# Two units of a query weight moved off POOL's scaling, and one weight split set ahead of a normed row

## The chip, the cores and the metric

The kernel runs on one core of a Trainium2 chip. The core has five engines that each take their own instructions in order: PE multiplies matrices, DVE and ACT work element by element and read the PSUM banks that PE writes, POOL works element by element in SBUF, and SP issues the transfers. The metric is the device time of one execution in microseconds (us), a median over runs.

## The reference

Two layers of an encoder on x of 512 rows and 1024 columns, in float32. Layer 0 mixes tokens with a banded attention (12 heads, each query sees 128 rows to either side) and a memory attention (4 heads over 256 memory rows); layer 1 has a global attention in place of the banded one. Each layer does this:

```
h    = rms_norm(x, g_mix_pre[i]);  proj = h @ w_in[i]      # q, k, v, q of the memory heads
o    = concat(token mixer, memory attention) @ w_o[i];     x = x + rms_norm(o, g_mix_post[i])
h    = rms_norm(x, g_ffn_pre[i]);  gu = h @ w_gate_up[i]
f    = (silu(gu[:, :2816]) * gu[:, 2816:]) @ w_down[i];    x = x + rms_norm(f, g_ffn_post[i])
```

## The kernel before

**Products of split operands.** Every float32 operand of a large product is split into a rounded part `hi` and a rest `lo = x - hi`, and `mm3` (L268) makes three matmuls from them (L270 to L272). A weight comes as a *unit* of 128x1024 elements: a transfer into `raw` (L224, three buffers), then `hi` (`whi`) and `lo` (`wlo`, four buffers each). The next transfer into a `raw` buffer can start once the unit in it has been split.

**Who splits.** `unit` has an argument `side`, a number of two bits that comes from the table `PACE`. In layer 0 the units of `w_in` and of the memory weights are scaled by the gain of the norm on the way (`g`). With the low bit set, POOL scales `raw` in place, 256 columns at a time (L236), and POOL also makes `lo` (L282); with the low bit clear, the scaling lies in the split itself (`split_scaled`, L286): `hi` by ACT (L292) or, with the high bit set, by POOL (L290), and `lo` by DVE (L293). With the low bit set, `hi` comes from ACT (L280) or, with the high bit, from POOL (L278).

**The first mixer.** `mixer` lays out pieces of work by due times from `PACE`. The query weights are eight units, `qw[2c + z]` for four blocks c of 256 columns and two halves z. While PE still projects queries and memory keys, it begins the scores (L548, L549) of the first heads. For a head, DVE adds the mask (L554), ACT takes the exponential (L560), POOL divides by the sums (`p`, L599) and PE transposes the result (L609). A tile of queries is scaled by ACT (L512), turned by four DVE operations (the rotary, L422 to L425), split by ACT (L280) and DVE (L284), and transposed (L524). The memory keys go through `keys` (L404): two batches of transposes (L409, L414), copied out by ACT (L411) and DVE (L415); the second batch has a single PSUM bank (`pv`).

**The start of the gate/up product.** In `ffn` the first two blocks f of 128 hidden columns are computed plainly, with four units (f, b), b for gate and up. They are laid between the last rows of the output projection. `plain` multiplies a unit; between the units stand `late.pop(2)` and `late.pop(3)`, which turn the third and fourth 128 rows of the normed h (`Forms.turn`: L149 transposes, L280 and L284 split, L159 copies, L162 subtracts). Row 3 of h is made by `post_norm`: DVE adds the residual (L742), ACT takes squares (L303), POOL makes the factor r with three operations on one column (L308, L313, L314), DVE multiplies (L756).

**The order.** PE's instructions stand as written. On the other engines a scheduler orders them by a priority that follows the order of the code; `high_priority(n)` moves what is recorded under it n places forward.

Of the kernel before, what the change touches and what calls it, by code (L numbers as in the profile page):

```python
# [31 lines left out]
WPART = 2  # L32
BIG = 1e37
NFILL = 3
LOTS = ((0, 8), (8, 14), (14, 22))

PACE = [{'lag': 1.692, 'vlag': 0.479, 'jstep': 0.213, 'kstep': 0.375, 'klag': 0.742, 'qoff': [0.212, 0.126, 0.099], 'qlag': 1.02, 'late': 0.6, 'moff': -0.235, 'mdur': 0.562, 'mlag': 0.697, 'kw': [0, 0, 2, 0], 'mw': [2, 1, 1, 0], 'qw': [1, 0, 0, 1, 3, 3, 3, 3], 'hoff': 0, 'ow': [10.3, 10.8, 12.2, 13.2], 'ox': 11.4, 'od': 0.3, 'hstep': 0.872, 'hlag': 1.742, 'hjstep': 0.135, 'hvlag': 0.751, 'owm': [0, 0, 0, 0, 0, 0, 0, 0], 'q0step': 0.27, 'q0off': -0.032, 'q0lag': 0.919, 'm0off': -0.078, 'm0dur': 0.002, 'm0lead': 1.887, 'mlead': 1.201, 'qlead': 0.921, 'q0lead': 1.555, 'qstep': 1.002, 'tw': [0, 0, 0, 0, 0, 0, 0, 0], 'h2off': 0}, {'lag': 1.824, 'vlag': 0.535, 'jstep': 0.218, 'kstep': 0.777, 'klag': 1.715, 'qoff': [-0.027, -0.162, -0.027], 'qlag': 1.189, 'late': 2.15, 'moff': -0.088, 'mdur': 0.384, 'mlag': 1.205, 'kw': [0, 0, 0, 0], 'mw': [0, 0, 0, 0], 'qw': [0, 0, 0, 0, 0, 3, 1, 1], 'hoff': 0, 'ow': [10.2, 10.7, 12.2, 13.2], 'ox': 11.3, 'od': 0.3, 'hstep': 0.946, 'hlag': 1.847, 'hjstep': 0.295, 'hvlag': 0.568, 'owm': [0, 0, 0, 0, 0, 0, 0, 0], 'q0step': 0.718, 'q0off': -0.018, 'q0lag': 1.136, 'm0off': -1.059, 'm0dur': 0.171, 'm0lead': 2.465, 'mlead': 3.162, 'qlead': 1.895, 'q0lead': 1.42, 'qstep': 0.998, 'tw': [0, 0, 0, 0, 0, 0, 0, 0], 'h2off': 0.016}]

# [139 lines left out]
class Trunk:  # L180
# [84 lines left out]
    def side(self, l, key, u):  # L265
        return PACE[l][key][u]

# [381 lines left out]
    def mixer(self, l, mkp, late, tokp):  # L649
        nc = self.nc  # L650
        pc = PACE[l]
        if l == 0:
# [112 lines left out]
    def heads_out(self, l, put, xw, xs, x0, dx):  # L765
# [7 lines left out]
        def part(k):  # L773
            if k % 4 == 0:
                self.th[k // 4] = [self.hp.tile([P, 4, S], F32R, tag=f"h{k // 4}{z}", name="th", bufs=1)
                                   for z in range(2)]
            self.split(self.th[k // 4][0][:, k % 4], self.th[k // 4][1][:, k % 4], self.tok[:, k],
                       self.side(l, "tw", k))

        def prod(k, t):  # L780
            if t == len(self.po):
                self.po.append(self.bank())
                if t == 2:
                    self.held = self.turns.pop()
            self.prod(self.po[t], self.heads, KD, k, t, self.wo[k // 2])

        for k in range(KD):
            put(max(xs[k], x0 + (NFILL * k - 1.5) * dx) if k < NH // 2 else xs[k], lambda k=k: part(k))
        for k in range(NH // 2):
            for t in range(NFILL):  # L790
                put(max(x0 + (NFILL * k + t) * dx, xs[k] + 0.001 * (t + 1)), lambda k=k, t=t: prod(k, t))

# [3 lines left out]
    def mix_out(self, l, forms, resid, dst):  # L796
# [3 lines left out]
        g, gn = self.gain(a["g_mix_post"][l], "gpost"), self.gain(a["g_ffn_pre"][l], "gpre")  # L800
        po = self.po + [self.bank() for _ in range(NT - NFILL)]
        self.turns.insert(1, self.held)
        w1 = []
        for u in range(4):
            for k in (2 * u, 2 * u + 1):
                for t in range(0 if k >= NH // 2 else NFILL, NT):
                    self.prod(po[t], self.heads, KD, k, t, self.wo[u])
# [97 lines left out]
    def ffn(self, l, pools, forms, late, done):  # L905
# [6 lines left out]
        w, raw, st = {}, {}, {}  # L912

        def units(f):
            w[f] = [self.unit(self.a["wgu"][l, f, b]) for b in range(2)]

        def plain(f, b, q, pg):
            c = slice(256 * q, 256 * q + 256)
            for k in range(KD):
                s = slice(k * P, (k + 1) * P)  # L920
                self.mm3(pg[b][:, c], w[f][b][0][:, s], w[f][b][1][:, s], forms.plain(0, k, q), forms.plain(1, k, q),
                         k == 0, k == KD - 1)
# [75 lines left out]
        def body(f, pos, nxt, nxt2, fill):  # L998
            d = st[f]
            x = d["x"]  # L1000
            seven(f, x, "c", 1, "S2", False)
            copy(f, "u2", x)
            y = self.tagged("t")[:, :256]
            seven(f, y, "c", 0, "nS1", True)
            copy(f, "p5", y)
            if nxt is not None:
                load_b(nxt)
                prep_c(nxt)
                p1(nxt)
            else:  # L1010
                fill[0]()
            seven(f, x, "b", 1 - 1, "S3", False)
            c = d["cc"] = temp("c")
            nc.vector.tensor_add(c[:, 256:], x, d["p5"])
            if nxt is not None:
                p2(nxt)
            else:
                fill[1]()
            if nxt2 is not None:
                prep_a(nxt2)  # L1020
            seven(f, y, "b", 1, "S4", False)
            nc.vector.tensor_add(c[:, :256], y, d["u2"])
            if nxt is not None:
                prep_b(nxt)
            seven(f, x, "d", 0, "A22", False)
            s = d["s"]
            nc.scalar.activation(s[:, 256:], x, AF.Silu)
            nc.vector.tensor_mul(s, s, c)
            F[f] = hidden(pos)
            nc.scalar.activation(F[f][0], s, AF.Copy, scale=-1.0)  # L1030
            nc.vector.scalar_tensor_tensor(F[f][1], s, -1.0, F[f][0].bitcast(F32), op0=OP.mult, op1=OP.subtract)
            if nxt is not None:
                prep_d(nxt)
            st.pop(f)

        pgs = []
        for f in range(2):
            units(f)
            pgs.append([self.bank() for _ in range(2)])
            for b in range(2):  # L1040
                plain(f, b, 0, pgs[f])
                if f == 0 and b == 1:
                    late.pop(2)()
                if f == 1 and b == 0:
                    late.pop(3)()
# [13 lines left out]

        for c, (f0, f1) in enumerate(LOTS):  # L1060
            fs = list(range(f0, f1))
# [21 lines left out]
            for i, f in enumerate(gs):  # L1083
                more = gs[i + 1:] + [None, None]
                body(f, f - f0, more[0], more[1], [first, second])
            if c < len(LOTS) - 1:
                self.down(get, self.a["wd"][l], fs, c, o, head)
# [158 lines left out]
```

## Time and profile before

| | us |
|---|---|
| median of 3 runs | 1124.72 |
| lowest, highest | 1124.1, 1125.98 |
| the profiled execution | 1125.38 |
| its span, first to last instruction | 1123.6 |
| PE busy | 1096.6 (98%) |
| DVE, ACT, POOL busy | 844.3 (75%), 660.8 (59%), 203.8 (18%) |

In 40 slices of the span the granted clock of PE is at its top (9 of 9 tenths) in every one. PE's digits are 9 in all slices but the first (8) and the last (7). POOL's digits are high only in the first seven slices, that is in the first 200 us, where it splits weights and scales probabilities.

### The profile page before, as it was taken

The numbers are of one execution on the slowest core, as the hardware profiler recorded it, in microseconds if no ns is written. First come the engines' busy times: TensorE is split into PE (matmuls) and PEld (weight loads), VectorE is DVE, ScalarE is ACT, GpSimd is POOL, SyncE is SP. The second block draws the span as 40 slices with busy tenths as digits, with TensorE's granted clock in tenths as the row PEclk, the third lists the DMA queues.
The fourth block names the chain that finished last, engine by engine and source line by source line (L and its number), as shares of the span: only waits on it lengthen the run. The fifth ranks groups of instructions, "written<-read, shape, count | busy, mean of one in ns | idle before, by whom it ended". The sixth has DMA issues, their size and how long they took to land.

```text
span 1123.6 us, 19533 instructions
## 1 busy us (share of the span) xinstructions
PE 1096.6 (98%) x7463; PEld 1003.6 (89%) x7463; DVE 844.3 (75%) x1431; ACT 660.8 (59%) x1343; POOL 203.8 (18%) x348
## 2 busy tenths in 40 slices
PE   8999999999999999999999999999999999999997
PEld 7889988899889989998898888878999899899985
DVE  5688885899557867885788998758996478669854
ACT  6678984666445634663467878756665255345631
POOL 5693331102000000000343543312000000000001
PEclk9999999999999999999999999999999999999999
DMA  6521015443753382325543221145136223423243
GB/s 237 194 81 47 20 57 206 169 132 114 243 180 112 112 283 76 112 79 195 179 150 113 76 76 39 38 150 188 39 113 217 65 76 114 149 62 103 85 166 112
DMA packets 38685, 139.29 MB, mean 124 GB/s; under 512 B 4416, under 2 KB 4800, under 8 KB 38464
## 3 DMA queue, kind: packets, MB, share of 16 engines
q1 hardware_dynamic: 38448, 137.91, 36.4%
q8 instruction: 58, 0.95, 0.3%
q14 instruction: 35, 0.29, 0.1%
q10 hardware_dynamic: 144, 0.14, 0.0%
HBM read 119.16 MB, written 18.87 MB: 123 GB/s over the span
## 4 chain that ended last, share of the span: by engine, by line
PE 68%; DVE 6%; ACT 3%; POOL 2%; issue 2%; DVEq 0%; POOLq 0%; ACTq 0%
PE ps L978 12%; PE ps L979 12%; PE ps L980 12%; PE ps L271 9%; PE ps L270 9%; PE ps L272 9%; PE tp L609 1%; PE o L624 1%; PE o L623 1%; PE s L548 1%; DVE nm L559 1%; PE s L549 1%; DVE wlo L284 1%; POOL r L299 1%; ACT whi L280 1%
## 5 line engine op out<-in xcount | busy, mean ns | idle before, releaser
L280 ACT ACTIVATE whi<-raw 128x1024 fp32r<-128x1024 f32 (+2 forms) x186 | 157.9, 863 | 185.2 <-PE ps L980 81.8
L284 DVE TENSOR_TENSOR wlo<-raw,whi 128x1024 fp32r<-128x1024 f32 (+2 forms) x178 | 175.9, 998 | 74.8 <-ACT whi L280 71.7
L978 PE MATMUL ps<-sf,whi 128*128 128x256 f32 x640 | 179.9, 281 | 0.2
L979 PE MATMUL ps<-sf,wlo 128*128 128x256 f32 x640 | 179.7, 281 | 0.0
L980 PE MATMUL ps<-sf,whi 128*128 128x256 f32 x640 | 179.7, 281 | 0.0
L270 PE MATMUL ps<-whi,f 128*128 128x512 f32 x352 | 137.2, 390 | 0.0
L271 PE MATMUL ps<-wlo,f 128*128 128x512 f32 x352 | 137.1, 390 | 0.0
L272 PE MATMUL ps<-whi,f 128*128 128x512 f32 x352 | 137.0, 389 | 0.0
L980 PE MATMUL ps<-a,whi 128*128 128x256 f32 x480 | 134.4, 280 | 0.0
L978 PE MATMUL ps<-a,whi 128*128 128x256 f32 x480 | 134.3, 280 | 0.0
L979 PE MATMUL ps<-a,wlo 128*128 128x256 f32 x480 | 133.8, 279 | 0.0
L978 PEld LDWEIGHTS ps<-sf,whi 128*128 128x128 f32 x640 | 121.1, 189 | 1.1 <-ACT p L984 0.6
L979 PEld LDWEIGHTS ps<-sf,wlo 128*128 128x128 f32 x640 | 121.4, 190 | 0.5
L980 PEld LDWEIGHTS ps<-sf,whi 128*128 128x128 f32 x640 | 121.4, 190 | 0.0
L308 POOL TENSOR_SCALAR e<-sso 128x1 f32<-128x1 f32 x8 | 3.4, 424 | 566.1 <-ACT junk L303 565.9
L270 PE MATMUL ps<-whi,hT 128*128 128x256 f32 (+1 forms) x320 | 98.8, 309 | 0.9 <-ACT whi L292 0.9
L271 PE MATMUL ps<-wlo,hT 128*128 128x256 f32 (+1 forms) x320 | 93.9, 294 | 2.6 <-DVE wlo L284 1.9
L599 POOL TENSOR_SCALAR p<-p,rd 128x256 f32<-128x256 f32 (+2 forms) x128 | 78.2, 630 | 99.8 <-DVE rd L596 50.3
L272 PE MATMUL ps<-whi,hT 128*128 128x256 f32 (+1 forms) x320 | 93.7, 293 | 0.0
L979 PEld LDWEIGHTS ps<-a,wlo 128*128 128x128 f32 x480 | 90.5, 188 | 0.2
L978 PEld LDWEIGHTS ps<-a,whi 128*128 128x128 f32 x480 | 90.4, 188 | 0.2
L980 PEld LDWEIGHTS ps<-a,whi 128*128 128x128 f32 x480 | 90.1, 188 | 0.0
(201 smaller groups left out, 2735.0 us busy)
## 6 DMA issues: line engine op xcount, KB each, us to landing
raw<-in_wgu_dram SPq DMA_DIRECT2D x48, 512.0 KB, 4.4
raw<-in_wd_dram SPq DMA_DIRECT2D x44, 512.0 KB, 4.4
rb<-in_wgu_dram SPq DMA_DIRECT2D x40, 512.0 KB, 3.6
raw<-in_wo_dram SPq DMA_DIRECT2D x17, 512.0 KB, 3.6
raw<-in_wq_dram SPq DMA_DIRECT2D x16, 512.0 KB, 5.0
xt<-x SPq DMA_DIRECT2D x12, 512.0 KB, 4.5
raw<-in_wm_dram SPq DMA_DIRECT2D x8, 512.0 KB, 4.3
x<-y SPq DMA_DIRECT2D x8, 512.0 KB, 3.0
```

What stands on the lines that cost most here:

```text
L270: mm(out, lh, rh, start=first, stop=False)
L271: mm(out, lh, rl, start=False, stop=False)
L272: mm(out, ll, rh, start=False, stop=last)
L280: nc.scalar.activation(hi, src, AF.Copy)
L284: nc.vector.tensor_sub(lo, src, hi.bitcast(F32))
L299: g.tensor_tensor(r, r, self.mhalf[:, :r.shape[1]], op=OP.pow)
L548: nc.tensor.matmul(s[:, :n], qi, hd["ka"]()[:, k0 * P:k1 * P], start=True, stop=False)
L549: nc.tensor.matmul(s[:, :n], qi, hd["kb"]()[:, k0 * P:k1 * P], start=False, stop=True)
L599: self.pooled = nc.gpsimd.tensor_scalar(hd["p"][z][:, :n], hd["p"][z][:, :n], rd[:, z:z + 1], 1.0, op0=OP.mult, op1=OP.mult)
L978: mm(out, wh[:, s], rh, start=start and k == 0, stop=False, skip_group_check=True)
L979: mm(out, wl[:, s], rh, start=False, stop=False, skip_group_check=True)
L980: mm(out, wh[:, s], rl, start=False, stop=k == 3, skip_group_check=True)
```

## The change

In layer 0's `qw`, unit 3 (c = 1, z = 1) goes from side 1 to side 0, and unit 4 (c = 2, z = 0) from side 3 to side 2. In `ffn`, in both layers, the unit (f, b) = (1, 1) is no longer recorded by `units(1)` but right behind it, with a priority moved forward by 150 places. The two `PACE` lines below are cut to the field that differs.

```diff
+EARLY = 150
...
-'qw': [1, 0, 0, 1, 3, 3, 3, 3]
+'qw': [1, 0, 0, 0, 2, 3, 3, 3]
...
         def units(f):
-            w[f] = [self.unit(self.a["wgu"][l, f, b]) for b in range(2)]
+            w[f] = [self.unit(self.a["wgu"][l, f, b]) for b in range(2 - f)]
...
         for f in range(2):
             units(f)
+            if f:
+                with self.tc.high_priority(EARLY):
+                    w[f].append(self.unit(self.a["wgu"][l, f, 1]))
             pgs.append([self.bank() for _ in range(2)])
```

PE's and SP's instructions stand as before. On POOL, in the first mixer, this is the stretch before. `raw_711` is unit 3, `raw_1087` unit 4, `raw_1139`, `raw_1597` and `raw_1630` are units 5 to 7; `k2_816` and `k2_841` are the memory keys, `p_888` the first head's probabilities.

```order
L236 TENSOR_SCALAR raw_711<-raw_711,cst_87 128x256 x4
L236 TENSOR_SCALAR raw_1087<-raw_1087,cst_87 128x256 x4
L282 TENSOR_TENSOR wlo_713<-raw_711,whi_712 128x512 x2
L278 TENSOR_SCALAR whi_1088<-raw_1087 128x512 x2
L282 TENSOR_TENSOR wlo_1089<-raw_1087,whi_1088 128x512 x2
L236 TENSOR_SCALAR raw_1139<-raw_1139,cst_87 128x256 x3
L402 TENSOR_SCALAR k2_816<-k2_816 128x4x64
L236 TENSOR_SCALAR raw_1139<-raw_1139,cst_87 128x256
L236 TENSOR_SCALAR raw_1597<-raw_1597,cst_87 128x256 x3
L278 TENSOR_SCALAR whi_1140<-raw_1139 128x512 x2
L402 TENSOR_SCALAR k2_841<-k2_841 128x4x64
L282 TENSOR_TENSOR wlo_1141<-raw_1139,whi_1140 128x512 x2
```

And this is the same stretch now, in which line numbers of this part of the code are one higher.

```order
L291 TENSOR_SCALAR whi_1088<-raw_1087,cst_87 128x256 x4
L237 TENSOR_SCALAR raw_1139<-raw_1139,cst_87 128x256 x4
L403 TENSOR_SCALAR k2_816<-k2_816 128x4x64
L237 TENSOR_SCALAR raw_1597<-raw_1597,cst_87 128x256
L279 TENSOR_SCALAR whi_1140<-raw_1139 128x512 x2
L403 TENSOR_SCALAR k2_841<-k2_841 128x4x64
L283 TENSOR_TENSOR wlo_1141<-raw_1139,whi_1140 128x512 x2
L237 TENSOR_SCALAR raw_1597<-raw_1597,cst_87 128x256 x3
L237 TENSOR_SCALAR raw_1630<-raw_1630,cst_87 128x256 x4
L600 TENSOR_SCALAR p_888<-p_888,rd_940 128x256
```

POOL loses the in-place scaling of two units, their two `lo` parts and the plain `hi` of one, and gets four scaled `hi` pieces. The `lo` parts of both units now stand on DVE, among the rotary of the query tile `qx_780` (the last one of c = 0); before, DVE had the first unit's four pieces there (`wlo_658`) and then the rotary.

```order
L294 SCALAR_TENSOR_TENSOR wlo_658<-raw_656,cst_87,whi_657 128x256 x4
L294 SCALAR_TENSOR_TENSOR wlo_713<-raw_711,cst_87,whi_712 128x256 x3
L294 SCALAR_TENSOR_TENSOR wlo_1089<-raw_1087,cst_87,whi_1088 128x256
L294 SCALAR_TENSOR_TENSOR wlo_713<-raw_711,cst_87,whi_712 128x256
L423 TENSOR_TENSOR rt_782<-qx_780,cst_87 128x4x8
L424 TENSOR_TENSOR rt_782<-qx_780,cst_87 128x4x8
L294 SCALAR_TENSOR_TENSOR wlo_1089<-raw_1087,cst_87,whi_1088 128x256
L425 TENSOR_TENSOR qx_780<-qx_780,cst_87 128x4x16
L294 SCALAR_TENSOR_TENSOR wlo_1089<-raw_1087,cst_87,whi_1088 128x256
L426 TENSOR_TENSOR qx_780<-qx_780,rt_782 128x4x16
L294 SCALAR_TENSOR_TENSOR wlo_1089<-raw_1087,cst_87,whi_1088 128x256
L285 TENSOR_TENSOR q2_787<-qx_780,q2_787 128x4x64
```

Eight pieces of `lo` are new on DVE, and the eighth stands ahead of the split of `q2_787`. On ACT, four scaled pieces of `whi_712` take the place of two plain ones, ahead of `qx_780`. At the start of the gate/up product of layer 0, DVE's order before is this; `wlo_3087` and `wlo_3093` belong to the units (1, 0) and (1, 1), `h_2976` is row 3, `a21` and `a22` are the split rows.

```order
L742 SCALAR_TENSOR_TENSOR y_2763<-y_2763,ro_2979,xt_2977 128x512 x2
L284 TENSOR_TENSOR wlo_3087<-raw_3085,whi_3086 128x1024
L756 SCALAR_TENSOR_TENSOR h_2976<-y_2763,r_2985,gain_2664 128x512 x2
L284 TENSOR_TENSOR wlo_3093<-raw_3091,whi_3092 128x1024
L284 TENSOR_TENSOR a21_2657<-tp_3067,a21_2656 128x4x128
L284 TENSOR_TENSOR a22_2655<-tp_3076,a22_2654 128x4x128
```

Now it is this, and layer 1 has the same exchange.

```order
L743 SCALAR_TENSOR_TENSOR y_2763<-y_2763,ro_2979,xt_2977 128x512 x2
L285 TENSOR_TENSOR wlo_3087<-raw_3085,whi_3086 128x1024
L285 TENSOR_TENSOR wlo_3093<-raw_3091,whi_3092 128x1024
L757 SCALAR_TENSOR_TENSOR h_2976<-y_2763,r_2985,gain_2664 128x512 x2
L285 TENSOR_TENSOR a21_2657<-tp_3067,a21_2656 128x4x128
L285 TENSOR_TENSOR a22_2655<-tp_3076,a22_2654 128x4x128
```

The `lo` of unit (1, 1) and the two halves of row 3 have changed places; nothing else moved there.

## Rows read from the trace of the kernel before

**Rows 1.** The page's first part: busy us (share of the span) and instructions.

```profile
PE 1096.6 (98%) x7463; PEld 1003.6 (89%) x7463; DVE 844.3 (75%) x1431; ACT 660.8 (59%) x1343; POOL 203.8 (18%) x348
```

**Rows 2.** PE's waits, whole span: line, waited for, us in total, times, longest.

```profile
PE tp L149 <- ACT a L159: 1.8, 2, 0.9
PE tp L149 <- DVE s L162: 1.2, 2, 0.6
```

**Rows 3.** PE's waits from 60 to 120 us.

```profile
PE tp L609 <- POOL p L599: 1.3, 2, 0.9
```

**Rows 4.** Timeline of PE: start us, us, engine, line, operation, count [idle before <-releaser].

```profile
54.54 0.39 PE L272 MATMUL ps<-whi,mT 128*128 128x512 f32 x1
...
60.77 0.46 PE L524 MATMUL tp<-identr,q 128*128 128x128 f32 x4
...
66.70 0.51 PE L414 MATMUL tp<-identr,k 128*128 128x128 f32 x4 [0.39 <-DVE kmb L415]
...
71.61 0.33 PE L609 MATMUL tp<-cst,p 128*128 128x128 f32 x1 [0.88 <-POOL p L599]
```

**Rows 5.** Timeline of POOL, 48 to 73 us.

```profile
48.42 3.88 POOL L236 TENSOR_SCALAR raw<-raw,cst 128x256 f32<-128x256 f32 x8 [6.87 <-DMA raw<-in_wq_dram]
54.45 2.60 POOL L282 TENSOR_TENSOR wlo<-raw,whi 128x512 fp32r<-128x512 f32 x2 [2.15 <-ACT whi L280]
...
58.21 2.73 POOL L282 TENSOR_TENSOR wlo<-raw,whi 128x512 fp32r<-128x512 f32 x2
...
66.23 2.53 POOL L282 TENSOR_TENSOR wlo<-raw,whi 128x512 fp32r<-128x512 f32 x2
...
71.08 2.23 POOL L599 TENSOR_SCALAR p<-p,rd 128x256 f32<-128x256 f32 x4
```

**Rows 6.** Timeline of DVE, 52 to 70 us.

```profile
52.68 1.69 DVE L293 SCALAR_TENSOR_TENSOR wlo<-raw,cst,whi 128x256 fp32r<-128x256 f32 x4 [0.73 <-ACT whi L292]
55.28 0.51 DVE L422 TENSOR_TENSOR rt<-qx,cst 128x32 f32<-128x32 f32 x1 [0.92 <-ACT qx L512]
...
55.93 1.20 DVE L424 TENSOR_TENSOR qx<-qx,cst 128x64 f32<-128x64 f32 x1
...
63.32 0.39 DVE L424 TENSOR_TENSOR qx<-qx,cst 128x64 f32<-128x64 f32 x1
...
65.87 0.68 DVE L415 CAST kmb<-tp 128x512 fp32r<-128x512 f32 x1
...
69.11 0.17 DVE L596 RECIPROCAL rd<-den 128x4 f32<-128x4 f32 x1
```

**Rows 7.** Timeline of ACT, 52 to 58 us.

```profile
52.14 1.71 ACT L292 ACTIVATE whi<-raw,cst 128x256 fp32r<-128x256 f32 x4 [0.76 <-PE ps L272]
...
57.81 0.42 ACT L280 ACTIVATE q<-qx 128x256 fp32r<-128x256 f32 x1 [1.95 <-DVE qx L425]
```

**Rows 8.** SP's issue after unit 3's split, and L224's transfers from 20 to 100 us.

```profile
57.07 0.33 SPq L224 DMA_DIRECT2D raw<-in_wq_dram  x1
...
DMA to landing us min/median/max: 3.5/3.6/7.5
```

**Rows 9.** Timeline of DVE, POOL and PE at layer 0's gate/up product.

```profile
210.33 1.22 DVE L284 TENSOR_TENSOR wlo<-raw,whi 128x1024 fp32r<-128x1024 f32 x1
...
210.66 0.94 POOL L308 TENSOR_SCALAR e<-ss 128x1 f32<-128x1 f32 x1 [2.90 <-ACT junk L303]
...
211.68 0.19 POOL L313 TENSOR_TENSOR r<-e,ss 128x1 f32<-128x1 f32 x1
...
212.53 1.42 DVE L756 SCALAR_TENSOR_TENSOR h<-y,r,gain 128x512 f32<-128x512 f32 x2 [0.99 <-POOL r L314]
...
213.86 1.22 DVE L284 TENSOR_TENSOR wlo<-raw,whi 128x1024 fp32r<-128x1024 f32 x1
...
215.00 1.28 DVE L284 TENSOR_TENSOR a<-tp,a 128x512 fp32r<-128x512 f32 x2
...
216.37 0.66 PE L149 MATMUL tp<-cst,h 128*128 128x128 f32 x4 [0.92 <-ACT a L159]
```

More of the change, by code (lines that the diff above doesn't have):

```diff
@@ L34 @@
 NFILL = 3
+EARLY = 150
 LOTS = ((0, 8), (8, 14), (14, 22))
-PACE = [{'lag': 1.692, 'vlag': 0.479, 'jstep': 0.213, 'kstep': 0.375, 'klag': 0.742, 'qoff': [0.212, 0.126, 0.099], 'qlag': 1.02, 'late': 0.6, 'moff': -0.235, 'mdur': 0.562, 'mlag': 0.697, 'kw': [0, 0, 2, 0], 'mw': [2, 1, 1, 0], 'qw': [1, 0, 0, 1, 3, 3, 3, 3], 'hoff': 0, 'ow': [10.3, 10.8, 12.2, 13.2], 'ox': 11.4, 'od': 0.3, 'hstep': 0.872, 'hlag': 1.742, 'hjstep': 0.135, 'hvlag': 0.751, 'owm': [0, 0, 0, 0, 0, 0, 0, 0], 'q0step': 0.27, 'q0off': -0.032, 'q0lag': 0.919, 'm0off': -0.078, 'm0dur': 0.002, 'm0lead': 1.887, 'mlead': 1.201, 'qlead': 0.921, 'q0lead': 1.555, 'qstep': 1.002, 'tw': [0, 0, 0, 0, 0, 0, 0, 0], 'h2off': 0}, {'lag': 1.824, 'vlag': 0.535, 'jstep': 0.218, 'kstep': 0.777, 'klag': 1.715, 'qoff': [-0.027, -0.162, -0.027], 'qlag': 1.189, 'late': 2.15, 'moff': -0.088, 'mdur': 0.384, 'mlag': 1.205, 'kw': [0, 0, 0, 0], 'mw': [0, 0, 0, 0], 'qw': [0, 0, 0, 0, 0, 3, 1, 1], 'hoff': 0, 'ow': [10.2, 10.7, 12.2, 13.2], 'ox': 11.3, 'od': 0.3, 'hstep': 0.946, 'hlag': 1.847, 'hjstep': 0.295, 'hvlag': 0.568, 'owm': [0, 0, 0, 0, 0, 0, 0, 0], 'q0step': 0.718, 'q0off': -0.018, 'q0lag': 1.136, 'm0off': -1.059, 'm0dur': 0.171, 'm0lead': 2.465, 'mlead': 3.162, 'qlead': 1.895, 'q0lead': 1.42, 'qstep': 0.998, 'tw': [0, 0, 0, 0, 0, 0, 0, 0], 'h2off': 0.016}]
@@ new lines @@
+PACE = [{'lag': 1.692, 'vlag': 0.479, 'jstep': 0.213, 'kstep': 0.375, 'klag': 0.742, 'qoff': [0.212, 0.126, 0.099], 'qlag': 1.02, 'late': 0.6, 'moff': -0.235, 'mdur': 0.562, 'mlag': 0.697, 'kw': [0, 0, 2, 0], 'mw': [2, 1, 1, 0], 'qw': [1, 0, 0, 0, 2, 3, 3, 3], 'hoff': 0, 'ow': [10.3, 10.8, 12.2, 13.2], 'ox': 11.4, 'od': 0.3, 'hstep': 0.872, 'hlag': 1.742, 'hjstep': 0.135, 'hvlag': 0.751, 'owm': [0, 0, 0, 0, 0, 0, 0, 0], 'q0step': 0.27, 'q0off': -0.032, 'q0lag': 0.919, 'm0off': -0.078, 'm0dur': 0.002, 'm0lead': 1.887, 'mlead': 1.201, 'qlead': 0.921, 'q0lead': 1.555, 'qstep': 1.002, 'tw': [0, 0, 0, 0, 0, 0, 0, 0], 'h2off': 0}, {'lag': 1.824, 'vlag': 0.535, 'jstep': 0.218, 'kstep': 0.777, 'klag': 1.715, 'qoff': [-0.027, -0.162, -0.027], 'qlag': 1.189, 'late': 2.15, 'moff': -0.088, 'mdur': 0.384, 'mlag': 1.205, 'kw': [0, 0, 0, 0], 'mw': [0, 0, 0, 0], 'qw': [0, 0, 0, 0, 0, 3, 1, 1], 'hoff': 0, 'ow': [10.2, 10.7, 12.2, 13.2], 'ox': 11.3, 'od': 0.3, 'hstep': 0.946, 'hlag': 1.847, 'hjstep': 0.295, 'hvlag': 0.568, 'owm': [0, 0, 0, 0, 0, 0, 0, 0], 'q0step': 0.718, 'q0off': -0.018, 'q0lag': 1.136, 'm0off': -1.059, 'm0dur': 0.171, 'm0lead': 2.465, 'mlead': 3.162, 'qlead': 1.895, 'q0lead': 1.42, 'qstep': 0.998, 'tw': [0, 0, 0, 0, 0, 0, 0, 0], 'h2off': 0.016}]
```

## The prediction

> **What bounds the kernel.** I read the busy shares first, then PE's waits, then the timelines around the waits that the change can touch. PE is busy for 1096.6 of the span of 1123.6 us [rows 1], so a change that adds or removes no matmul can win only from the 27 us in which PE stands idle. Two kinds of wait lie beside the change. At the start of the gate/up product PE stalls twice in each layer at the transposes of L149: the waits for L159 sum to 1.8 us in two times, those for L162 to 1.2 us in two times [rows 2], so 1.5 us a layer. In the first mixer PE waits 1.3 us for POOL's division of the first head's probabilities [rows 3] and, five us earlier, 0.39 us for DVE's copy `kmb` of the memory keys [rows 4].
>
> **The mixer part: what goes.** POOL's `p` of the first head starts at 71.08 us, with no idle time in front of it [rows 5], while DVE had its factor `rd` at 69.11 + 0.17 = 69.28 [rows 6]. The wait in rows 3 is therefore POOL's backlog. The change takes from POOL eight scalings (3.88 us), two pairs of `lo` (2.60 and 2.73 us) and one plain `hi`, and adds four scaled `hi` pieces, which I price like scalings, 3.88 / 8 = 0.485 us each [rows 5]. POOL then reaches `p` near 69 us and waits for DVE; PE wants it at 71.61 - 0.88 = 70.73 [rows 4]. So 1.28 us of waiting goes.
>
> **What comes on DVE and ACT.** DVE gets eight more pieces of `lo` at 1.69 / 4 = 0.42 us, 3.4 us in all [rows 6]; ACT gets four scaled pieces, 1.71 us, less the plain ones that they replace. ACT's part lies in front of the 1.95 us in which it waited for the rotary [rows 7] and costs nothing; without that cover it would cost at most 1.71. DVE's part has this cover: in the old order DVE idled 0.92 us before the rotary [rows 6], and the rotary was stretched. L424 took 1.20 us at 55.93, and 0.39 at 63.32, where POOL was scaling and made no `lo` [rows 6]. Its long case ends at 57.13, just behind POOL's second `lo` piece (54.45 + 2.60 = 57.05 [rows 5]); L422 at 55.28 ends at 55.79, just behind POOL's first (half of the pair, 55.75). I read that as a rule of this trace: a DVE operation with two inputs in SBUF that meets a POOL operation there waits until it ends. `kmb`, at 65.87 under the third pair, reads one input from PSUM and takes its ordinary 0.68. Two of POOL's three pairs go, and with them about 2 us of this stretching, so 3.4 us of new pieces meet 0.9 + 2 us of freed time and some waiting behind POOL's short pieces. POOL's new `hi` can start only when PE has finished with an old buffer of memory weights, at 54.54 + 0.39 = 54.93 [rows 4], so it runs to about 57, piece by piece ahead of DVE. I put the last query split of block 0 at 59.6 to 60.1 us, as before within 0.3.
>
> **What is late next.** The third pair, unit 5's `lo`, moves. It stood at 66.23 [rows 5], behind the rotary of the next query tile (L424 at 63.32 [rows 6]). Now POOL comes to it sooner: unit 6 can be loaded when DVE ends unit 3, near 56.7 in place of 57.07, and lands 3.6 us later [rows 8], at 60.3; one scaling (0.5), unit 5's `hi` (1.2) and the key copy (0.4) follow, so the pair starts between 62.1 and 63.2. It then lies on the rotary, which starts near 63.0. By the rule above L422 waits for the first piece and L424 for the second, so the rotary ends at about 65.4, not 64.2; ACT's split, DVE's split and one mask operation follow, and `kmb` slips from 65.87 to about 67.0. PE's L414 starts at 67.85, not 66.70. That costs 1.15 us (0.7 to 1.95 over the range of starts) ahead of the 1.28 us that go. I take the sum, -0.1 us, with ends of -1.3 (no collision) and +0.7.
>
> **The gate/up part.** On paper it is worth a microsecond a layer. DVE idled 0.99 us before row 3's multiplication at 212.53, waiting for r; the `lo` of (1, 1) then ran at 213.86 and pushed the split of `a21` to 215.00, on which L159 and PE's 0.92 us hang [rows 9]. With `lo` set into the idle time that split would start 1.05 us earlier, and both PE waits of that place would shrink by 1.05 us together.
>
> But the operations that make r are on POOL. While DVE ran the `lo` of (1, 0) from 210.33 to 211.55, POOL's one-column L308 at 210.66 took 0.94 us and ended at 211.60; its like L313, at 211.68, took 0.19 [rows 9]. In layer 1 the same L308 takes 0.94 us as well, again to the end of a `lo`. So POOL is held as DVE was above. In the new order the `lo` of (1, 1) follows at once at about 211.5, and L313 meets it at 211.68. It would end near 212.8, not 211.87. From L313's start to the multiplication there are 212.53 - 211.68 = 0.85 us, 0.66 of it after L313's end; the multiplication then starts at 213.45 and the split of `a21` 1.33 later (213.86 - 212.53), at 214.8. Gain: 0.2 us a layer, -0.4 in all. Ends: -2.1 for two layers if POOL is not held, +0.2 if DVE takes both `lo` ahead of L308 and the chain of three then starts late. I take the near end, since the rows show the holding at this very place.
>
> The Trainium skill states this as a rule ("SBUF — State Buffer", Who interferes with whom): a vector instruction with two inputs in SBUF contends with a POOL instruction that reads SBUF, and whoever comes first holds the shared port for its whole instruction. Rows 9 agree (0.94 against 0.19 us). By the rule the gate/up part yields -0.4 us, without it -2.1.
>
> **Sum.** Against the profiled execution's own 1125.38 us (span 1123.6, 1.78 around it): -0.1 - 0.4 = -0.5, so 1124.88. That execution lies 0.66 above the median of 1124.72; on the median the forecast is 1124.2.
>
> **Rivals.**
> - *POOL is not held in the gate/up part.* For it: POOL's chain may reach L313 before DVE has taken up the second `lo`, if L308 is let in between the two. Against it: the second `lo` waits for nothing and would start at 211.5, L313 at 211.68. Time: 1124.72 - 2.1 - 0.1 = 1122.5.
> - *No collision in the mixer.* If the pair starts after the rotary, or the rotary goes first, `kmb` is not late: 1124.72 - 1.3 - 0.4 = 1123.0. For it: the old rotary did run ahead of the pair. Against it: everything ahead of the pair on POOL has become shorter.
> - *DVE becomes the bound at 55 to 62 us, slower.* Each of five new pieces waits for a whole POOL piece of 0.485 us, 2.4 us more; the last query split of block 0 ends at 62.0, and PE's transposes of it, which stand at 60.77 [rows 4], start 1.3 us late. This decides as soon as the split is over 1 us later than before. For it: DVE has no idle time left in that stretch. Against it: beside POOL's scalings L424 took 0.39 us and not 1.20 [rows 6], so short POOL pieces hold DVE little. Time: 1124.2 + 1.3 = 1125.5.
>
> **How the numbers follow.** Chances: the forecast 0.60, the first rival 0.15, the second 0.12, the third 0.13. A difference under 0.2%, 2.25 us, can't be told from none. Faster by more needs a time under 1122.47: half of the first rival, and the little in which the first two hold together, 0.12. Slower by more needs 1126.97, beyond the third rival with the ends of the others, 0.05. The rest, 0.83, is within. The range goes from the first rival with a good part of the second's gain, 1121.9, to the third with a little more, 1125.8.
>
> **What would show it.** In the changed profile: PE's wait for `p` of the first head is gone; L414's wait for `kmb` is 1 to 2 us; L424 of the rotary near 63 us takes over a microsecond; the `lo` of (1, 1) lies directly behind that of (1, 0), L313 beside it takes about 1.1 us, and row 3's multiplication starts about 0.9 us later than in rows 9; PE's wait for L159 shrinks from 0.92 to about 0.7. I am wrong in the gate/up part if L313 takes 0.2 us and the wait is gone, and in the mixer if L414 waits no longer than 0.4 us or PE waits for the query transposes near 61 us.

## The result and the profile after

The changed kernel takes 1126.35 us (median of 20 runs, 1124.86 to 1127.22), the kernel before 1124.70 in the same session (20 runs, 1123.96 to 1125.98). The ratio is 1.0013, with a 95% interval of 1.0007 to 1.0019: slower by 0.8 to 2.1 us. The forecast was 1124.2, and the range ended at 1125.8.

The page of the profiled execution (span 1125.4 us, before 1123.6) answers to [rows 1]. The second row is the granted clock of PE in 40 slices.

```profile
PE 1099.2 (98%) x7463; PEld 1007.0 (89%) x7463; DVE 846.5 (75%) x1439; ACT 661.5 (59%) x1345; POOL 199.1 (18%) x338
...
PEclk9989999999999999999999999999999999999999
```

PE is busy 2.6 us longer with the same 7463 matmuls, and one slice, the third, shows a lower clock. So in this execution the loss is not in the idle time: that went from 27.0 to 26.2 us. PE's waits from 60 to 120 us, answering to [rows 3], begin with this one, and POOL's `p` is no longer among them.

```profile
PE tp L415 <- DVE kmb L416: 2.5, 1, 2.5
```

PE's timeline there, answering to [rows 4]:

```profile
60.02 0.46 PE L525 MATMUL tp<-identr,q 128*128 128x128 f32 x4
...
68.08 0.72 PE L415 MATMUL tp<-identr,k 128*128 128x128 f32 x4 [2.52 <-DVE kmb L416]
...
69.15 0.41 PE L273 MATMUL ps<-whi,hT 128*128 128x256 f32 x1
...
74.23 0.36 PE L549 MATMUL s<-ka,qT 128*128 128x384 f32 x1
```

The wait for `kmb` grew from 0.39 to 2.52 us, by 2.13. And the matmuls of 256 columns behind it start 0.21 us apart, where they start 0.12 us apart elsewhere. The stretches of the windows view tell why (length, busy us and count of each engine, granted clock, DMA share, GB/s):

```profile
66.00:68.00 2.00, 0.00 (x0) 0.00 (x0) 1.99 (x7) 1.94 (x7) 2.00 (x5) 0.85 0.79 244
68.00:74.00 6.00, 5.92 (x29) 5.95 (x30) 3.19 (x14) 3.37 (x11) 2.62 (x6) 0.50 0.02 6
74.00:76.00 2.00, 2.00 (x18) 1.97 (x17) 1.22 (x5) 1.48 (x5) 0.00 (x0) 0.94 0.00 0
```

PE stood idle, and the granted clock fell to 0.50, its lower level (1.2 GHz), until about 74 us. In the kernel before it was 1.00 in all of these stretches. There, the matmul that answers to the one at 74.23 came 3.52 us behind L414's start at 66.70 [rows 4]:

```profile
70.22 0.34 PE L548 MATMUL s<-ka,qT 128*128 128x384 f32 x1
```

Now the same stretch takes 74.23 - 68.08 = 6.15 us: 2.63 us lost to the clock alone, about as much as PE's busy time grew.

POOL, answering to [rows 5], and DVE, answering to [rows 6], show where `kmb` lost its time.

```profile
62.61 2.53 POOL L283 TENSOR_TENSOR wlo<-raw,whi 128x512 fp32r<-128x512 f32 x2
65.14 3.37 POOL L237 TENSOR_SCALAR raw<-raw,cst 128x256 f32<-128x256 f32 x7
71.42 2.11 POOL L600 TENSOR_SCALAR p<-p,rd 128x256 f32<-128x256 f32 x4 [2.92 <-DVE rd L597]
```

```profile
58.44 0.61 DVE L285 TENSOR_TENSOR q<-qx,q 128x256 fp32r<-128x256 f32 x1
...
62.60 1.35 DVE L424 TENSOR_TENSOR rt<-qx,cst 128x32 f32<-128x32 f32 x1
63.98 1.25 DVE L425 TENSOR_TENSOR qx<-qx,cst 128x64 f32<-128x64 f32 x1
...
67.25 0.68 DVE L416 CAST kmb<-tp 128x512 fp32r<-128x512 f32 x1
```

The pair of unit 5 lies on the rotary: two operations of DVE that took 0.18 us (the row below, from before) and 0.39 us [rows 6] beside scalings last 1.35 and 1.25 us, each to the end of one of POOL's pieces.

```profile
63.10 0.18 DVE L423 TENSOR_TENSOR rt<-qx,cst 128x32 f32<-128x32 f32 x1
```

POOL now waits 2.92 us for `rd` and is no longer the one that PE waits for. What that is worth shows from start to start of PE's matmuls, first before, then now:

```profile
72.33 0.33 PE L609 MATMUL tp<-cst,p 128*128 128x128 f32 x1 [0.40 <-POOL p L599]
72.42 0.36 PE L270 MATMUL ps<-whi,hT 128*128 128x256 f32 x1
```

```profile
74.60 0.38 PE L610 MATMUL tp<-cst,p 128*128 128x128 f32 x2
74.74 0.36 PE L271 MATMUL ps<-whi,hT 128*128 128x256 f32 x1
```

From the matmul of 384 columns at 70.22 to the next product it was 72.42 - 70.22 = 2.20 us, and from the one at 74.23 it is 74.74 - 74.23 = 0.51: 1.7 us less, where the two waits sum to 1.28 (0.88 and 0.40). A wait is counted from the end of the record before it, while in an unbroken row the next matmul starts ahead of that end (0.12 us apart, in records of 0.28, for 256 columns), so that each of the two waits is counted some 0.2 us too short. For `kmb` this makes no difference, since PE waited there before and after.

At the gate/up product of layer 0, answering to [rows 9] (DVE, POOL and PE):

```profile
212.65 2.36 DVE L285 TENSOR_TENSOR wlo<-raw,whi 128x1024 fp32r<-128x1024 f32 x2
...
212.97 2.08 POOL L309 TENSOR_SCALAR e<-ss 128x1 f32<-128x1 f32 x1 [1.75 <-ACT junk L304]
...
215.14 0.19 POOL L314 TENSOR_TENSOR r<-e,ss 128x1 f32<-128x1 f32 x1
...
215.99 1.42 DVE L757 SCALAR_TENSOR_TENSOR h<-y,r,gain 128x512 f32<-128x512 f32 x2 [0.98 <-POOL r L315]
...
218.69 0.66 PE L150 MATMUL tp<-cst,h 128*128 128x128 f32 x4 [0.91 <-ACT a L160]
```

Both `lo` run back to back, POOL's one-column `e` stands through both of them, and the chain of r starts when the second has ended. DVE's idle time in front of row 3's multiplication is still there (0.98, before 0.99), only later, and PE's wait is 0.91 (before 0.92). Layer 1 reads the same, 0.92. This part gave nothing and cost nothing.

The span of this one profile grew by 1.8 us: 2.6 of busy time, less 0.8 of idle time. The idle time is 2.1 more at `kmb`, 1.3 less at `p`, and about 1.1 less in the first 20 us, where both programs are alike. The profile of before has a wait there which most others don't have:

```profile
PE ps L270 <- ACT whi L292: 0.9, 1, 0.9
```

The remaining 0.5 us are several waits that shrank by a tenth or two each.

### The profile page after: what moved, and what is told of

It is laid out like the page before. It is cut to its first block, busy times and chain, and to the rows that moved or that the text cites. A ratio compares the mean times of both kernels' runs of the same rounds, so it can differ in the third digit from the quotient of the medians.

```text
span 1125.4 us, 19536 instructions
## 1 busy us (share of the span) xinstructions
PE 1099.2 (98%) x7463; PEld 1007.0 (89%) x7463; DVE 846.5 (75%) x1439; ACT 661.5 (59%) x1345; POOL 199.1 (18%) x338
## 4 chain that ended last, share of the span: by engine, by line
PE 68%; DVE 6%; ACT 3%; POOL 2%; issue 1%; DVEq 0%; POOLq 0%; ACTq 0%
PE ps L979 12%; PE ps L981 12%; PE ps L980 12%; PE ps L272 9%; PE ps L271 9%; PE ps L273 9%; PE tp L610 1%; PE o L625 1%; PE o L624 1%; PE s L549 1%; PE s L550 1%; DVE nm L560 1%; POOL r L300 1%; ACT whi L281 1%; ACT junk L304 0%
```

## The experiments

The theory after the result: the mixer part makes the whole loss, by the collision of POOL's third pair with the rotary, and PE's stall then costs a second time through the clock; the gate/up part is worth nothing, since DVE's `lo` holds POOL's chain. Rivals: the gate/up part loses; `kmb` is late because DVE has more to do; the clock falls for a reason of its own.

**Each part alone.** The kernel before with the new table alone:

```diff
-'qw': [1, 0, 0, 1, 3, 3, 3, 3]
+'qw': [1, 0, 0, 0, 2, 3, 3, 3]
```

> The kernel before with the mixer part of the change alone (query units 3 and 4 in their new forms, the gate/up split as before). Theory: the whole loss is made in the mixer, so this runs at the time of the changed kernel, 1126.3 us (1125.7 to 1126.9): PE waits 2 to 2.6 us for kmb at the second batch of key transposes, waits nothing for the first p, and TensorE's granted clock is near 0.5 (1.2 GHz) for some 6 us behind that wait. Rival: the loss comes from the gate/up part, then the time is that of the kernel before or under it, 1123.4 to 1124.7.

And the changed kernel with the old table, so with the exchange in the gate/up product alone:

> The changed kernel with the old table of query units: the gate/up part alone. Theory: it yields nothing, 1124.7 us within 0.4: DVE runs the two lo of (1,0) and (1,1) back to back (2.3 to 2.4 us), POOL's one-column e of the last row takes about 2.1 us beside them, and PE's waits at the gate/up transposes stay 0.9 and 0.6 us in each layer. First rival (the step of the prediction, POOL comes in between): 0.2 us a layer, 1124.3, e at 0.9 us and the next POOL operation at 1.1. Second rival (POOL is not held): 1122.6, with both waits of PE gone.

The mixer alone took 1126.08 us, ratio 1.0012 (1.0003 to 1.0020): the whole loss. PE's row and the stretch behind it:

```profile
68.44 0.51 PE L414 MATMUL tp<-identr,k 128*128 128x128 f32 x4 [2.58 <-POOL raw L236]
```

```profile
68.00:74.00 6.00, 5.56 (x35) 5.55 (x35) 3.76 (x16) 4.03 (x12) 2.53 (x5) 0.72 0.01 3
```

The wait is put down to a POOL scaling of a query weight here, which the transposes don't read. PE goes on 0.14 us behind the end of DVE's `kmb`, 67.62 + 0.68 = 68.30 us, as it does in the changed kernel (68.08, behind 67.93). DVE:

```profile
62.57 1.28 DVE L422 TENSOR_TENSOR rt<-qx,cst 128x32 f32<-128x32 f32 x1
63.78 1.32 DVE L423 TENSOR_TENSOR rt<-qx,cst 128x32 f32<-128x32 f32 x1
...
67.62 0.68 DVE L415 CAST kmb<-tp 128x512 fp32r<-128x512 f32 x1
```

The clock is down for a shorter time, and the stretch to the matmul that answers to the one at 74.23 takes 5.00 us in place of 3.52: 1.48 lost.

The exchange alone took 1124.55 us, ratio 1.0002 (0.9993 to 1.0011): no difference that an interval of 1 us to either side can show. Its profile shows both forms of the holding, one in each layer (POOL):

```profile
209.77 0.94 POOL L309 TENSOR_SCALAR e<-ss 128x1 f32<-128x1 f32 x1 [2.89 <-ACT junk L304]
210.79 1.05 POOL L314 TENSOR_TENSOR r<-e,ss 128x1 f32<-128x1 f32 x1
...
777.72 2.08 POOL L309 TENSOR_SCALAR e<-ss 128x1 f32<-128x1 f32 x1 [1.76 <-ACT junk L304]
```

In layer 0, POOL came in between the two `lo`, then its next operation was held for 1.05 us, and PE's wait was 0.65 in place of 0.92 us: this is the step that the prediction took. In layer 1 it stood through both. Over the seven profiles of kernels that have this exchange, 11 of 14 passages are of the second form and 3 of the first, all three in layer 0.

**The pair set later.** One edit takes away the collision and nothing else: an edge for the scheduler that sets the `lo` of unit 5 behind `kmb` in POOL's order, so behind the seven scalings.

```diff
+            if pair == ("wq", 0, 2, 1):
...
+                last = nc.gpsimd.tensor_tensor(lo[:, c0:c1], raw[:, c0:c1], hi[:, c0:c1].bitcast(F32), op=OP.subtract).ins
+                self.tc.add_manual_dep(last, self.kmb.name, mybir.DependencyInfo(
+                    mybir.DependencyClass.NoSync, mybir.DependencyReason.DATA), reason="order")
```

> The changed kernel with one pair of POOL instructions, the lo of query unit 5, set behind the seven scalings of units 6 and 7, so behind the rotary of the next query tile; every other queue is as in the changed kernel. Theory: kmb was late because that pair lay on the rotary. Then the rotary's four operations take about 0.4 us each, kmb runs 1.5 to 2 us earlier than in the changed kernel, PE's wait for it falls from 2.5 to 0.4 us or less, the granted clock stays at 1.00, the first p is still on time, and the time is 1124.7 - 1.3 = 1123.4 us (1122.9 to 1124.2). Rival: kmb is late because DVE has eight more lo pieces to do; then PE still waits 1 to 2.5 us for it and the time stays at 1125.5 to 1126.5.

It took 1122.94 us (11 runs; before 1124.68), ratio 0.9985 (0.9976 to 0.9993): faster than both kernels. DVE, POOL and PE:

```profile
62.14 0.45 DVE L430 TENSOR_TENSOR rt<-qx,cst 128x32 f32<-128x32 f32 x1
62.51 0.18 DVE L431 TENSOR_TENSOR rt<-qx,cst 128x32 f32<-128x32 f32 x1
62.72 0.39 DVE L432 TENSOR_TENSOR qx<-qx,cst 128x64 f32<-128x64 f32 x1
...
65.14 0.68 DVE L421 CAST kmb<-tp 128x512 fp32r<-128x512 f32 x1
```

```profile
65.45 2.54 POOL L242 TENSOR_TENSOR wlo<-raw,whi 128x512 fp32r<-128x512 f32 x2
68.67 2.28 POOL L607 TENSOR_SCALAR p<-p,rd 128x256 f32<-128x256 f32 x4 [0.68 <-DVE rt L431]
```

```profile
65.96 0.51 PE L420 MATMUL tp<-identr,k 128*128 128x128 f32 x4 [0.60 <-DVE kmb L421]
```

DVE's queue is the same, instruction for instruction, with all eight added pieces; so these are not what makes `kmb` late. `kmb` runs 2.1 us earlier, PE waits 0.60 us, and the clock is 1.00 throughout. The step from the changed kernel is 1126.35 - 1122.94 = 3.4 us: 2.52 - 0.60 = 1.9 of waiting; the rest, 1.5, is put down to the clock.

The same with the old order in the gate/up product:

> The mixer part alone with the pair set later (the gate/up split as in the kernel before). Theory: the gain of the kernel with the pair set later is all the mixer's, and the gate/up part is worth nothing, so this runs at its time: 1122.9 us (1122.4 to 1123.5), with PE's waits at the gate/up transposes 0.92 and 0.60 us. Rival: the gate/up part had a share in that gain; then 1123.5 to 1124.2.

It took 1122.90 us, ratio 0.9986 (0.9977 to 0.9995), with waits of 0.92 and 0.60 us at the gate/up transposes, as with the exchange: no share of the gate/up part in the gain is seen, and the gain is the mixer's.

**The stall filled.** Twenty matmuls stand ahead of the waiting transposes.

```diff
+        if self.fill and (n, t) == (4, 1):
+            for _ in range(self.fill):
+                nc.tensor.matmul(self.spare, self.hslice(0, 0, 0, P), self.hslice(0, 0, 0, 256), start=True, stop=True,
+                                 skip_group_check=True)
```

> The changed kernel with 20 extra matmuls of 256 columns on PE ahead of the key transposes that wait for kmb; their product is never read, nothing else moves. Each takes 0.12 us at 2.4 GHz, so they fill 2.4 of the 2.5 us in which PE stands. Theory: the fall of the granted clock is owed to PE standing idle there; with the stall filled the clock stays at 1.00 from 68 to 74 us, the matmuls behind take 0.28 and not 0.41 us, kmb still comes as late as in the changed kernel, and the time is 1126.35 - 2.6 = 1123.7 us (1123.2 to 1124.5). Rival: the clock falls for a reason of its own (work done earlier, power); then the granted clock is near 0.5 again and the time stays at 1126.3 or rises.

They write over part of a query product that is still in its bank, which the expectation overlooked, so one query tile of this kernel is wrong. PE, and the stretch behind:

```profile
68.48 0.51 PE L420 MATMUL tp<-identr,k 128*128 128x128 f32 x4 [0.17 <-POOL raw L237]
```

```profile
68.00:74.00 6.00, 5.83 (x50) 5.62 (x49) 4.87 (x18) 4.69 (x15) 2.53 (x6) 1.00 0.02 6
```

The transposes come as late as in the changed kernel (68.48 against 68.08), but the clock stays at 1.00: the fall belongs to PE's standing idle. The time is 1125.44 us, 0.9 below the changed kernel and not 2.6. The size in the expectation was taken from one profile; the next two show that it was a long one. The 0.9 us are still less than the 1.3 to 1.5 us which the clock costs there; in part PE pays elsewhere, since it waits 0.4 us for `tl` at L631, where the changed kernel waits 0.2 (its L625). The intervals, of 0.7 us to either side for the changed kernel and 1 us for this one, leave room for the rest.

**Two more profiles of the changed kernel.**

> The changed kernel once more, one look at its clock. Theory: the wait for kmb is 2.4 to 2.6 us in every execution and the granted clock falls behind it each time, but it stays down for a time that differs, 3 to 7 us (3.3 us in the kernel with the mixer part alone, 6.6 in the first profile of the changed kernel), at 0.21 us in place of 0.12 us for a matmul of 256 columns: 1.3 to 2.7 us. Rival: the fall belongs to that one execution, and the clock is 1.00 here.

> The changed kernel once more, one look, for the spread: as for the look before, the granted clock near 0.5 for 3 to 7 us behind the wait for kmb, costing 1.3 to 2.7 us; by the rival it is 1.00.

The waits were 2.50 and 2.23 us, the times 1125.94 and 1126.01, and the clock fell in both. The first one's stretches:

```profile
68.00:70.00 2.00, 1.63 (x12) 1.66 (x13) 1.43 (x5) 1.53 (x6) 1.24 (x3) 0.79 0.36 143
70.00:72.00 2.00, 2.00 (x13) 2.00 (x12) 1.28 (x7) 1.07 (x3) 0.81 (x2) 0.50 0.00 0
72.00:74.00 2.00, 2.00 (x15) 1.97 (x14) 1.05 (x4) 1.39 (x3) 1.29 (x3) 0.86 0.00 0
```

From the transposes to the matmul that answers to the one at 74.23 it is 73.36 - 68.37 = 4.99 us here and 72.76 - 67.90 = 4.86 in the other: 1.47 and 1.34 us lost, against 2.63 in the first profile. So the clock costs 1.3 to 1.5 us in three of four executions, 2.6 in one.

**Unit 5 taken from POOL as well.**

```diff
-'qw': [1, 0, 0, 0, 2, 3, 3, 3]
+'qw': [1, 0, 0, 0, 2, 2, 3, 3]
```

> The changed kernel with unit 5 taken from POOL as well: POOL scales its hi pieces and DVE makes its lo in four pieces, so that no lo pair of POOL is left in this stretch. Theory: with no pair on the rotary, kmb comes at least as early as with the pair set later, less four pieces of 0.42 us where they fall ahead of it; PE waits for kmb 0.5 to 2 us, the clock stays at 1.00 if that wait is under 1.5 us, and the time is 1123 to 1124.7 us. Rival: DVE's extra pieces are what makes kmb late; then its wait is 2.5 us or more and the time 1126.3 us or above.

1125.34 us, ratio 1.0006 (0.9996 to 1.0015; one run of eleven, of 1528.34 us, is left out of it): slower than was expected and faster than the rival says. DVE and PE:

```profile
61.54 1.31 DVE L294 SCALAR_TENSOR_TENSOR wlo<-raw,cst,whi 128x256 fp32r<-128x256 f32 x2 [1.03 <-POOL whi L291]
```

```profile
65.00 0.41 PE L549 MATMUL s<-ka,qT 128*128 128x384 f32 x1 [1.54 <-DVE vm L294]
...
68.04 0.51 PE L415 MATMUL tp<-identr,k 128*128 128x128 f32 x4 [0.49 <-DVE kmb L416]
```

Here a `lo` piece stands at the head of DVE's queue and waits 1.03 us for POOL's `hi`, with the splits of the memory values (`vm`) queued behind it, and PE waits 1.54 us for those. The two stalls together are 2.0 us and the clock stays at 1.00 behind them, so that what was won at `p` (1.7 us) is lost again.

**A `lo` that reads one operand from SBUF.** In the kernel with the exchange alone, the `lo` of (1, 1) is a copy; the subtraction is left out, so the product is not that of the reference:

```diff
-                    w[f].append(self.unit(self.a["wgu"][l, f, 1]))
...
+                    nc.vector.tensor_copy(lo[:, 1017:], raw1[:, 1017:])
+                    one = raw1[:, :1023].rearrange("p (a b) -> p a b", a=3)[:, :, :339]
+                    nc.vector.tensor_copy(lo[:, :1017].rearrange("p (a b) -> p a b", a=3), one)
```

> The gate/up part alone (mixer as before), in which DVE's lo of (1,1), a subtraction of two SBUF operands, is replaced by a copy of one SBUF operand of nearly the same length (1017 columns and 7); the subtraction is left out. Theory: POOL's one-column operations are held only by a DVE operation with two operands in SBUF. Then e is held by the lo of (1,0) as before (0.94 us), the two operations behind it take 0.19 and 0.55 us although the copy runs beside them, row 3's multiplication does not start later against e than before (1.9 us behind e's start), the split of a21 comes 1 us earlier, PE's waits at the gate/up transposes shrink by 1 us in each layer, and the time is 1124.55 - 2 = 1122.6 us (1122.0 to 1123.3). Rival: any DVE operation holds POOL, or the chain is late for another reason; then e or the next operation takes over a microsecond, PE's waits stay at 0.9 and 0.6 us, and the time stays at 1124.5.

1122.25 us, ratio 0.9978 (0.9968 to 0.9987), so 2.3 under the exchange with the subtraction. POOL and DVE of layer 0:

```profile
209.68 0.97 POOL L309 TENSOR_SCALAR e<-ss 128x1 f32<-128x1 f32 x1 [2.89 <-ACT junk L304]
210.73 0.19 POOL L314 TENSOR_TENSOR r<-e,ss 128x1 f32<-128x1 f32 x1
```

```profile
210.58 1.20 DVE L1048 CAST wlo<-raw 128x1017 fp32r<-128x1017 f32 x1
211.70 1.40 DVE L757 SCALAR_TENSOR_TENSOR h<-y,r,gain 128x512 f32<-128x512 f32 x2
```

The copy takes as long as the subtraction (1.20 against 1.22 us) and starts at the same place, but `e` ends with the first `lo`, and the next operation takes 0.19 us beside the copy. The multiplication starts 2.02 us behind `e` and without idle time, and PE's wait for the split of `a21` is gone in both layers (0.92 each). The Trainium skill ("SBUF — State Buffer", Who interferes with whom) says that a DVE instruction with at most one SBUF input, outside the modes in which it uses two ports, leaves POOL alone; this run agrees.

**The same from PSUM, with the subtraction kept.** On top of the pair set later, ACT copies the raw weights into PSUM, and DVE subtracts from there.

```diff
+                        with self.tc.issue_after(self.square):
+                            nc.scalar.activation(pr, raw1[:, c], AF.Copy)
+                        nc.vector.tensor_sub(lo[:, c], pr, hi[:, c].bitcast(F32))
```

> The kernel with the pair set later, and in the gate/up product DVE's lo of (1,1) made in two halves of 512 columns from a copy of the raw weights that ACT puts into PSUM behind the two squares of the last row (two copies of some 0.5 us): the same subtraction, with one operand in SBUF. Theory: such a subtraction doesn't hold POOL, so e is held by the lo of (1,0) alone (0.94 us), the next two POOL operations take 0.19 and 0.55 us, the first half fills DVE's idle time, the second pushes row 3's multiplication by 0.5 to 0.6 us, and the 1.22 us of the old place are saved: 0.65 us a layer, PE's 0.92 us wait falls to about 0.3. Time 1122.9 - 1.3 = 1121.6 us (1120.8 to 1122.4). Rival: ACT's copies delay the squares or the splits behind them, or the halves hold POOL all the same; then 1122.9 or above.

1123.43 us, ratio 0.9992 (0.9983 to 1.0001): no gain over 1122.94. DVE:

```profile
210.54 0.75 DVE L764 SCALAR_TENSOR_TENSOR h<-y,r,gain 128x512 f32<-128x512 f32 x1 [0.99 <-POOL r L320]
211.21 1.28 DVE L1058 TENSOR_TENSOR wlo<-pr,whi 128x512 fp32r<-128x512 f32 x2
212.40 0.74 DVE L764 SCALAR_TENSOR_TENSOR h<-y,r,gain 128x512 f32<-128x512 f32 x1
```

The scheduler set both halves behind the first half of the multiplication, so the 0.99 us of idle time stayed empty and PE waited 0.98 us. The run doesn't test what it was made for; whether a subtraction from PSUM brings the copy's gain stays open.

## Why the prediction was wrong

The step that failed is the price of a stall of PE. The prediction put the time that the clock loses behind it at nothing, and two further costs, the collision and the gate/up part, were taken too low, by 1.0 and 0.4 us.

- **The clock.** This term is missing in the prediction: a stall of PE was priced at its own length, and PE's busy time was taken as fixed ("can win only from the 27 us in which PE stands idle"). With stalls of 2.2 to 2.6 us the granted clock fell to 0.50, which cost 1.3 to 1.5 us more in three profiles and 2.6 in the fourth. Without it the other terms sum to +0.4 us, which would be lost in the noise.
- **`p`.** Right in the mechanism: the wait is gone, POOL reaches `p` early and waits for `rd`. The term was 0.4 us too small: 1.28, the sum of two waits, against 1.7 from start to start. With the pair set later this gain shows in the time, 1.7 us in all.
- **Cover on DVE.** Right: the last query split of block 0 ran at 58.44 to 59.05 us, ahead of its transposes at 60.02. The third rival's place did not become the bound.
- **The collision.** The mechanism was right, the term was mis-sized. The prediction said 1.15 us for L414, with 1.95 as the far end; it is 2.13. The pair was put at 62.1 to 63.2 and started at 62.61. But this execution ran about 0.75 us ahead of that of before (the query transposes at 60.02, not 60.77), so in the time of before the pair started at 63.36, past the late end, while the rotary started at 62.26 + 0.75 = 63.01, as was forecast. It met the rotary's second and third operations and held the rotary to the end of the whole pair, 65.14, with one more operation (0.42) still to come. The cost hangs little on which operations are met: with the mixer part alone these were the first and the second (1.28 and 1.32 us), and over the four profiles PE's wait grew by 1.84 to 2.19 us.
- **The gate/up part.** That POOL is held was right; the step behind it was not. The prediction let POOL's L308 in between the two `lo` and took 0.2 us a layer for it. That is the rarer form (0.92 - 0.65 = 0.27). Its far end, "DVE takes both `lo` ahead of L308", is what happens in 11 of 14 passages, and there the wait stays 0.92. In the rows of before the two `lo` never stood back to back, so they showed that POOL is held, and not that the next DVE operation goes ahead of a POOL operation that is already waiting.
- **The sum.** In place of -0.1 - 0.4: -1.7 for `p`, +2.1 for `kmb`, +1.3 to +1.5 for the clock, 0 for the gate/up part, so +1.7 to +1.9 us. Measured +1.65 (0.8 to 2.1). The range ended 0.55 us too early, since nothing in its slow end let a stall cost more than its length.
- **The second rival** (no collision, 1123.0) is what the kernel with the pair set later does: 1122.94.

## What to carry to other kernels

When work is taken from an engine in front of others, ask where its remaining long operations land: here a pair of 2.5 us moved some three microseconds forward onto four short operations that the bound engine was waiting for, and one edge in the scheduler's order turned +1.65 us into -1.7. A stall of the bound engine is not priced at its length alone: compare the granted clock behind it, and where there is a choice try two short stalls for a long one (1.54 and 0.49 us left the clock at 1.00 here, in one profile). Filling a gap on DVE that waits for a chain on POOL with DVE work that has two operands in SBUF gained nothing here, or at most 0.3 us a layer; a copy with one such operand did fill the gap.

## What the runs showed of the hardware

- Behind PE waits of 2.23 to 2.58 us the granted clock fell to 0.50 in all four profiles; in two of them it was lower already before PE went on (0.85 and 0.92 in 66 to 68 us, with a wait of 2.52 and 2.23); in the other two it was 1.00 there, 0.79 and 0.84 in the next 2 us, and 0.50 behind them. Behind the wait of 1.54 us (unit 5 taken as well) and that of 0.60 us (the pair set later) the rows show 1.00. How long it stays down differs from one execution to the next at the same place, and with the stall filled by matmuls it did not fall.
- DVE and POOL hold each other, but not evenly. DVE's short operations came in between POOL's two `lo` pieces (one waited for each); POOL's one-column operation, 0.33 us behind the start of DVE's first `lo`, mostly stood through the second as well: 2.08 us in 11 of 14 passages, 0.94 in three.
